# The state products of a group in one run, and padded decay tiles, in a Mamba-2 and attention trunk

## The chip, the cores and the metric

The kernel runs on one core of one Trainium2 chip. The metric is the device time of one execution in microseconds (us); lower is better. The engines are called PE (TensorE, matrix products and transposes), DVE (VectorE), ACT (ScalarE), POOL (GpSimd) and SP (SyncE, which issues the transfers).

## The reference

The input x has 512 positions of 1024 channels. A Mamba-2 layer is followed by one K/V projection and a differential attention layer; all is float32. The change lies in the Mamba-2 layer, of which these lines matter (G = 8 groups, R = 4 heads a group, head dimension 64, state 128; the kernel uses chunks of 128 positions, so NQ = 4 of them):

```python
zxbcdt = rms_norm(x, norm_g) @ w_in            # z, x/B/C and dt
xbc = silu(causal_depthwise_conv(xbc, conv_w, conv_b))
dt = softplus(dt_raw + dt_bias)
# per chunk, per group:
acs = cumsum(a * dt);  decay = exp(where(causal, acs[l] - acs[s], -inf))
y_diag = einsum((C @ B.T) * decay, x * dt)
y_off  = einsum(C, state) * exp(acs)
state  = state * exp(acs[-1]) + einsum(B, x * dt * exp(acs[-1] - acs))
# after all chunks:
y = y_diag + y_off + d_skip * x
u = y * silu(z);  u = u * rsqrt(mean(u * u over the group) + EPS) * gate_norm_g
x = x + u @ w_out
```

## The kernel before, in words

**Dense products.** The projections go through PE as three products in place of one (`mm3`): a weight is split into a head `whi` (made on ACT, `head`, line 144) and a rest `wlo` (made on DVE, `rest`, line 150), an activation likewise (`a_hi`, `a_lo`; `yh`, `yl`), and whi x hi, wlo x hi and whi x lo are summed. One product is 128x512 or a part of it. The weights come in segments: z0 g0 g1 z1 g2 g3 z2 g4 o0 g5 z3 g6 g7 o1 o2 o3, where z is the gate, g one group's x, B and C, and o the out-projection of two groups, in two halves. Segments are fetched some ahead of their use. In the trace the products are named pz, pg and po with their four token blocks; those of an out-projection segment `o3`, first half, have the names po3_0_0 to po3_0_3 and take the weights whi30 and wlo30. The second half of o3 has the weights whi31 and wlo31, which are placed in the two buffers of the decays, tag "dec" (line 137).

**The scan.** `ssd(g)` (from line 567) does one group, with these steps: B times C of each chunk (pcb, PE); transposes of B and x (pbt, pxt, PE) and from them bt (ACT), xdt = x dt and dx = d_skip x (DVE); xe, xdt weighted to a chunk's end, for three chunks (POOL, line 595); the product of pcb and the decays (DVE, into `dec`); the state products psA (chunks 0 and 1) and psB (chunk 2), full float32, each shown as two records; from these the states hst, in turns of ACT, POOL and DVE; the products pyd within a chunk, 64 records; the products of C with the states, po1 (chunk 1) and po2 (chunks 2 and 3), which the trace names po<-hst,xc; tmp, these times exp(acs) (DVE); dx + tmp (POOL, line 644); the gating with zs (DVE); the squares for the mean (ACT, with a read of the accumulator each); v and a chain of nine small operations of 128x4 for the inverse root (DVE, names y_i, y_y, y_c); the scaling tmp<-dx,y_y (ACT, in group 7 half of it on DVE); the transposes pyt back (PE); yh (ACT) and yl (DVE), which are the out-projection's activation. The residual x_tok takes each finished block of po (DVE).

**What sets the order.** Each engine takes its instructions in one order, which is fixed when the program is built. `tile.TileContext` (with `schedule_with_timeline_sim=True`) merges the stream of dense segments with the instructions of `ssd(g)` by a simulated timeline. What is issued through the wrapper `Ordered` (line 45; `T` is PE's) while its `on` is set stays in the order in which it was written, relative to the others kept so; `ssd(7)` is issued with high priority. So a small edit in `ssd` can move many instructions on all engines. Tiles are placed by pools: `bp` and `bp2` hold those of the scan, and a tile of odd length shifts the place of those behind it. At the places of the diff the kernel has a tile `shift` of 96 floats in `bp2`, and `dec` has N_DEC = 2056 floats.

Of the kernel before, what the change touches and what calls it, by code (L numbers as in the profile page):

```python
# [9 lines left out]
F32 = mybir.dt.float32  # L10
F32R = mybir.dt.float32r
# [6 lines left out]
P = 128  # L18
# [21 lines left out]
N_PAR = 203  # L40

N_DEC = R * NQ * P + 2 * R


class Ordered:
# [18 lines left out]
def trunk(ctx, tc, x, x_t, par, w_dt, w_in, w_out, w_kvqg, w_bo, d_skip, lam_qk, fin_g, out):  # L64
    nc = tc.nc
    V, A, T = (Ordered(tc, e) for e in (nc.vector, nc.scalar, nc.tensor))
# [14 lines left out]
    def ss_bank(name):  # L81
        turns[0] += 1
        tag = "mm" if turns[0] % turns[1] >= 3 else "ss"
        return psum.tile([P, 512], F32, tag=tag, name=name, bufs=3 if tag == "ss" else 4)
# [22 lines left out]
    def source(seg):  # L107
        kind, a, b = seg
        if kind == "z":
            return w_in[a * 6 + b], [prm[:, C_GA + 4 * b + i:C_GA + 4 * b + i + 1] for i in range(4)]  # L110
        if kind == "g":
            return w_in[(a // 2) * 6 + 2 + (a % 2) * 2 + b], [prm[:, C_GA + 4 * b + i:C_GA + 4 * b + i + 1] for i in range(4)]
        if kind == "o":
            return w_out[a * 2 + b], [prm[:, C_GG + 4 * a + i:C_GG + 4 * a + i + 1] for i in range(4)]
        if kind in "bc":
            return w_bo[a], None
        name = f"v{a}" if kind == "v" else a
        at = C_GK if kind in "vk" else C_GB
        return w_kvqg[[i for i in ORDER_B if i[0] not in "bc"].index(name)], [prm[:, at + i:at + i + 1] for i in range(8)]
# [5 lines left out]
    def load(i):  # L125

        seg = segs[i]
        src, gains = source(seg)
        nk = 8 if seg[0] in "vkqt" else 4
        w = 2048 // nk  # L130
        raw = begun[i] if i in begun else wp.tile([P, nk, w], F32, tag="raw", name=f"raw{i}", bufs=2)
        fetched[0] += 1

        def split():

            pool, tags = (bp, ("dec", "dec")) if seg == ("o", 3, 1) else (wp, ("whi", "wlo"))
            if pool is bp:
                hi, lo = (pool.tile([P, N_DEC], F32R, tag=tag, name=f"{n}{i}", bufs=2)[:, 0:2048].rearrange("p (k n) -> p k n", k=nk)
                          for n, tag in zip(("whi", "wlo"), tags))
            else:  # L140
                hi, lo = (pool.tile([P, nk, w], F32R, tag=tag, name=f"{n}{i}", bufs=2) for n, tag in zip(("whi", "wlo"), tags))
            ready[seg] = (hi, lo)

            def head(k):
                if gains:
                    A.activation(hi[:, k, :], raw[:, k, :], AF.Copy, scale=gains[k])
                else:
                    A.copy(hi[:, k, :], raw[:, k, :])

            def rest(k):  # L150
                if gains:
                    V.scalar_tensor_tensor(out=lo[:, k, :], in0=raw[:, k, :], scalar=gains[k],
                                           in1=hi[:, k, :].bitcast(F32), op0=ALU.mult, op1=ALU.subtract)
                else:
                    V.tensor_tensor(out=lo[:, k, :], in0=raw[:, k, :], in1=hi[:, k, :].bitcast(F32), op=ALU.subtract)

            return [(head, rest, k) for k in range(nk)]

        if i == 0:

            nc.sync.dma_start(raw[:, 0, :], src[:, 0:w])
            for n in range(2):
                nc.sync.dma_start(xt[0][:, 0, n * 256:(n + 1) * 256], x_t[:, 0, n * 256:(n + 1) * 256])
            nc.sync.dma_start(raw[:, 1, :], src[:, w:2 * w])
            for n in range(2):
                nc.sync.dma_start(xt[0][:, 1, n * 256:(n + 1) * 256], x_t[:, 1, n * 256:(n + 1) * 256])
            for k in range(2, 4):
                nc.sync.dma_start(raw[:, k, :], src[:, k * w:(k + 1) * w])
                nc.sync.dma_start(xt[1][:, k - 2, :], x_t[:, k, :])

            nxt, (src1, _) = wp.tile([P, nk, w], F32, tag="raw", name="raw1", bufs=2), source(segs[1])
            begun[1] = nxt
            for i in range(2, 4):
                nc.sync.dma_start(xt[i], x_t[:, 2 * i:2 * i + 2, :])
                nc.sync.dma_start(nxt[:, 2 * i - 4:2 * i - 2, :].rearrange("p k n -> p (k n)"), src1[:, (2 * i - 4) * w:(2 * i - 2) * w])
            nc.sync.dma_start(prc[:], par[:, C_CB:N_PAR])
        elif i not in begun:
            nc.sync.dma_start(raw.rearrange("p k n -> p (k n)"), src)
        return split
# [177 lines left out]
    bp = bctx.enter_context(tc.tile_pool(name="bp", bufs=1))  # L357
    bp2 = bctx.enter_context(tc.tile_pool(name="bp2", bufs=2))

    bp2.tile([P, 96], F32, name="shift", bufs=1)  # L360

    zt = {}
    yT = {}
# [55 lines left out]
    for k in range(KD):  # L419
        for c in range(NQ):  # L420
            T.matmul(ps_dt[c * H:(c + 1) * H, 0:P], lhsT=dtw_raw[:, k, :], rhs=xt[k // 2][:, k % 2, c * P:(c + 1) * P],
                     start=k == 0, stop=k == KD - 1)
# [125 lines left out]
    def decays(gs):  # L548

        for g in gs:  # L550
            hs = slice(R * g, R * g + R)
            both = bp.tile([P, N_DEC], F32, tag="dec", name=f"dec{g}", bufs=2)
            dec = both[:, 0:R * NQ * P].rearrange("p (h c l) -> p h c l", h=R, c=NQ)
            een = both[:, R * NQ * P:].rearrange("p (h q) -> p h q", h=R)
            nc.sync.dma_start(both[:, 0:R * NQ * P],
                                acs_d[hs].rearrange("h c l -> (h c l)").partition_broadcast(P))
            GP.tensor_copy(een, dec[:, :, 1:3, P - 1])
            for h in range(R):
                GP.tensor_tensor(out=dec[:, h], in0=dec[:, h], in1=acs_tok[:, :, R * g + h].unsqueeze(2).to_broadcast([P, NQ, P]), op=ALU.subtract)
                GP.affine_select(out=dec[:, h], in_=dec[:, h], compare_op=ALU.is_ge, fill=-BIG, base=0,  # L560
                                 pattern=[[0, NQ], [1, P]], channel_multiplier=-1)
            decs[g] = (dec, een, both)

        for g in gs:
            A.activation(decs[g][2], decs[g][2], AF.Exp)

    def ssd(g):
        bc, cc, x0, x1 = conv_out.pop(g)
        xc = (x0, x1)
        dec, een, _ = decs.pop(g)  # L570
# [29 lines left out]
        hsf = hst.rearrange("p c h e -> p c (h e)")  # L600
        psA = ss_bank(f"psA{g}")
        T.on = True
        for c in range(2):
            T.matmul(psA[:, c * 256:(c + 1) * 256], lhsT=bt[:, c, :], rhs=xe[:, c].rearrange("p h e -> p (h e)"), start=True, stop=True)
        A.copy(hsf[:, 0], psA[:, 0:256])
        GP.tensor_tensor(out=hst[:, 1], in0=hst[:, 0], in1=een[:, :, 0:1].to_broadcast([P, R, HD]), op=ALU.mult)
# [21 lines left out]
        if g % 2 and g < G - 1:  # L628
            decays((g + 1, g + 2))

        po1 = ss_bank(f"po1{g}")
        T.matmul(po1[:, 256:512], lhsT=cc[:, P:2 * P], rhs=hsf[:, 0], start=True, stop=True)
        po2 = ss_bank(f"po2{g}")
        for c in (2, 3):
            T.matmul(po2[:, (c - 2) * 256:(c - 1) * 256], lhsT=cc[:, c * P:(c + 1) * P], rhs=hsf[:, c - 1], start=True, stop=True)
        V.tensor_tensor(out=tmp[:, 1], in0=po1[:, 256:512].rearrange("p (h e) -> p h e", e=HD),
                        in1=eacs_tok[:, 1, hs].unsqueeze(2).to_broadcast([P, R, HD]), op=ALU.mult)
        V.tensor_tensor(out=tmp[:, 2:4], in0=po2.rearrange("p (c h e) -> p c h e", h=R, e=HD),
# [20 lines left out]
        n = 2 if g == G - 1 else NQ  # L659
# [6 lines left out]
        yT[g] = (yh, yl)  # L666

    decays((0, 1))
    dense[0] = stream_a()
    for g in range(G):  # L670
        until(f"g{g}")
        if g < G - 1:
            ssd(g)
        else:
            with tc.high_priority():
                ssd(g)
# [282 lines left out]
    def half(t, n):  # L959
        hs = slice(n * 512, (n + 1) * 512)  # L960
        return x_tok[:, t, hs], fg[:, hs], ot[t][:, hs], out[t * P:(t + 1) * P, hs]
# [123 lines left out]
    y, f, o, dst = half(3, 0)  # L1085
# [8 lines left out]
    y, f, o, dst = half(3, 1)  # L1094
# [68 lines left out]
```

## Time and profile before

| | before |
|---|---|
| median of 3 runs | 709.59 us (709.17 to 709.61) |
| profiled execution | 709.26 us |
| its span (first to last instruction) | 707.5 us |
| instructions | 10916 |
| PE busy | 697.5 us, 99% |
| DVE / ACT / POOL busy | 519.5 / 430.1 / 111.7 us |

The times of the profile count from the start of the span. A row of a timeline has the start, the duration of the whole row, the engine, the line and operation, the tile written and the tiles read with the buffer numbers left out, the shapes and a count of like instructions in sequence; a bracket names idle time before the row and what ended it. Matmuls overlap: a step is read from one start to the next, not from a duration. All operations that go through a recording helper have one line, 55 in the kernel before and 56 after.

### The profile page before, as it was taken

How to read it: one execution, taken by the hardware profiler on the slowest of the kernel's cores; microseconds unless marked ns; L12 is line 12 of the kernel's file. 1: busy time of each engine (PE TensorE's matmuls, PEld its weight loads, DVE VectorE, ACT ScalarE, POOL GpSimd, SP SyncE). 2: the span in 40 equal slices, each digit the busy share in tenths (PEclk: the TensorE clock that was granted, in tenths of full speed). 3: DMA queues.
4: the chain of work that ended last, by engine and by line, in shares of the span. 5: the costliest groups of instructions: out<-in, count | busy, mean ns of one | idle time of the engine just before them, and what ended most of it. 6: DMA issues, size and time to landing. Idle time of an engine off the chain costs nothing.

```text
span 707.5 us, 10916 instructions
## 1 busy us (share of the span) xinstructions
PE 697.5 (99%) x4030; PEld 590.8 (84%) x4030; DVE 519.5 (73%) x1197; ACT 430.1 (61%) x955; POOL 111.7 (16%) x158
## 2 busy tenths in 40 slices
PE   9999999999999999999999999999999999999996
PEld 7777888888888888888888879888988998899885
DVE  5479964889579569568997856566767757785886
ACT  6739672764744537538535367676667766756556
POOL 0009421503306024050110101000000000000002
PEclk9999999999999999999999999999999999999999
DMA  8644313333133331331221311412211221122003
GB/s 303 246 151 152 120 59 127 113 120 120 60 119 120 120 120 60 119 120 59 73 100 68 120 60 36 152 60 93 87 61 60 75 105 59 61 101 80 31 0 120
DMA packets 13493, 70.88 MB, mean 100 GB/s; under 512 B 1792, under 2 KB 3328, under 8 KB 6016
## 3 DMA queue, kind: packets, MB, share of 16 engines
q1 hardware_dynamic: 13008, 69.90, 27.6%
q8 instruction: 32, 0.52, 0.3%
q10 hardware_dynamic: 432, 0.28, 0.1%
q14 instruction: 21, 0.17, 0.1%
HBM read 68.02 MB, written 2.16 MB: 99 GB/s over the span
## 4 chain that ended last, share of the span: by engine, by line
PE 88%; ACT 4%; DVE 3%; DMA 3%; issue 1%; SPq 0%; ACTq 0%; DVEq 0%
PE pg L55 20%; PE po L55 16%; PE pz L55 9%; PE pt L55 7%; PE pv L55 6%; PE pq L55 6%; PE pk L55 6%; PE pb L55 3%; DMA raw<-in_w_in 3%; PE sc L55 3%; PE pyd L55 2%; PE pc L55 2%; ACT whi L55 1%; PE pxt L55 1%; PE psA L55 1%; PE pyt L55 1%
## 5 line engine op out<-in xcount | busy, mean ns | idle before, releaser
L55 DVE SCALAR_TENSOR_TENSOR wlo<-raw,prm,whi 128x512 fp32r<-128x512 f32 (+1 forms) x256 | 150.8, 637 | 56.1 <-ACT whi L55 55.6
L55 ACT ACTIVATE whi<-raw,prm 128x512 fp32r<-128x512 f32 (+1 forms) x256 | 136.8, 607 | 62.8 <-issue 13.1
L55 PE MATMUL pg<-a_hi,whi 128*128 128x512 f32 x256 | 102.2, 399 | 0.4 <-ACT zs L55 0.3
L55 PE MATMUL pg<-a_lo,whi 128*128 128x512 f32 x256 | 101.1, 395 | 0.0
L55 PE MATMUL pg<-a_hi,wlo 128*128 128x512 f32 x256 | 100.0, 396 | 0.0
L55 DVE SCALAR_TENSOR_TENSOR xc<-pg,prc,xc 128x511 f32<-128x511 f32 (+2 forms) x96 | 69.9, 739 | 7.5 <-ACT xc L55 7.1
L55 PEld LDWEIGHTS pg<-a_hi,whi 128*128 128x128 f32 x256 | 48.1, 188 | 10.5 <-ACT zs L55 0.6
L55 PEld LDWEIGHTS pg<-a_hi,wlo 128*128 128x128 f32 x256 | 48.1, 188 | 9.8
L55 PEld LDWEIGHTS pg<-a_lo,whi 128*128 128x128 f32 x256 | 48.1, 188 | 9.6
L55 PE MATMUL po<-whi,yh 128*128 128x512 f32 x128 | 50.8, 397 | 0.4 <-ACT yh L55 0.4
L55 PE MATMUL po<-wlo,yh 128*128 128x512 f32 x128 | 50.8, 397 | 0.0
L55 PE MATMUL po<-whi,yl 128*128 128x512 f32 x128 | 50.1, 395 | 0.0
L55 PE MATMUL pz<-wlo,a_hi 128*128 128x512 f32 x128 | 49.3, 394 | 0.0
L55 PE MATMUL pz<-whi,a_hi 128*128 128x512 f32 x128 | 48.9, 396 | 0.0
L55 PE MATMUL pz<-whi,a_lo 128*128 128x512 f32 x128 | 48.8, 390 | 0.0
L968 POOL TENSOR_TENSOR ot<-x_tok,fg 128x512 f32<-128x512 f32 x4 | 5.0, 1290 | 246.4 <-DVE x_tok L55 246.4
L55 ACT ACTIVATE s<-s,mx 128x128 f32<-128x128 f32 (+3 forms) x64 | 35.5, 556 | 9.7 <-DVE mx L55 9.3
L55 ACT ACTIVATE xc<-pg,prc 128x512 f32<-128x512 f32 x32 | 24.8, 776 | 24.5 <-DVE pg L55 19.6
L595 POOL TENSOR_TENSOR xe<-xdt,tok 128x256 f32<-128x256 f32 x24 | 14.1, 614 | 161.5 <-DVE xdt L55 161.5
L55 DVE CUSTOM_DVE_ANT_0 s<-sc,bias 128x128 f32<-128x128 f32 (+3 forms) x64 | 29.3, 487 | 12.3 <-PE sc L55 11.8
L55 PE MATMUL pv<-whi,b_hi 128*128 128x256 f32 x128 | 36.9, 289 | 0.0
L55 PE MATMUL pv<-whi,b_lo 128*128 128x256 f32 x128 | 36.2, 283 | 0.0
(238 smaller groups left out, 1676.5 us busy)
## 6 DMA issues: line engine op xcount, KB each, us to landing
raw<-in_w_in SPq DMA_DIRECT2D x22, 1024.0 KB, 4.9
raw<-in_w_kvqg SPq DMA_DIRECT2D x16, 1024.0 KB, 4.8
dec<-acs_d SPq DMA_DIRECT2D x8, 1024.0 KB, 4.8
raw<-in_w_out SPq DMA_DIRECT2D x8, 1024.0 KB, 4.7
raw<-in_w_bo SPq DMA_DIRECT2D x4, 1024.0 KB, 4.7
x_tok<-in_x SPq DMA_DIRECT2D x4, 512.0 KB, 9.0
out<-ot SPq DMA_DIRECT2D x6, 256.0 KB, 2.3
raw<-in_w_in SPq DMA_DIRECT2D x4, 256.0 KB, 4.7
```

Source lines behind the costliest of these rows:

```text
L55: i = op(*args, **kw)
L595: GP.tensor_tensor(out=xe[:, c], in0=xdt[:, c], in1=toe_tok[:, c, hs].unsqueeze(2).to_broadcast([P, R, HD]), op=ALU.mult)
L968: GP.tensor_tensor(out=o, in0=y, in1=f, op=ALU.mult)
```

## The change

Four edits:

- the state products are issued as chunk 1 then chunk 0 (psA), and po2 (chunk 3, then 2) is issued ahead of po1, these three now inside a stretch that is kept in written order;
- the decays' tiles get 2176 floats in place of 2056, of which the same 2056 are used; o3's second half in the same buffers too;
- the tile `shift` has 112 floats in place of 96 and moves from the pool `bp2` to `bp`;
- the argument dynamic_dma_scratch_size of the program is 1024 where it had its default, which moves the tiles by 15360 bytes a partition.

```diff
+N_DEC_PAD = 2176
...
-                hi, lo = (pool.tile([P, N_DEC], F32R, tag=tag, name=f"{n}{i}", bufs=2)[:, 0:2048].rearrange("p (k n) -> p k n", k=nk)
+                hi, lo = (pool.tile([P, N_DEC_PAD], F32R, tag=tag, name=f"{n}{i}", bufs=2)[:, 0:2048].rearrange("p (k n) -> p k n", k=nk)
...
-    bp2.tile([P, 96], F32, name="shift", bufs=1)
+    bp.tile([P, 112], F32, name="shift")
...
-            both = bp.tile([P, N_DEC], F32, tag="dec", name=f"dec{g}", bufs=2)
+            both = bp.tile([P, N_DEC_PAD], F32, tag="dec", name=f"dec{g}", bufs=2)[:, 0:N_DEC]
...
-        for c in range(2):
+        for c in (1, 0):
             T.matmul(psA[:, c * 256:(c + 1) * 256], lhsT=bt[:, c, :], rhs=xe[:, c].rearrange("p h e -> p (h e)"), start=True, stop=True)
...
+        po2 = ss_bank(f"po2{g}")
+        T.on = True
+        for c in (3, 2):
+            T.matmul(po2[:, (c - 2) * 256:(c - 1) * 256], lhsT=cc[:, c * P:(c + 1) * P], rhs=hsf[:, c - 1], start=True, stop=True)
         po1 = ss_bank(f"po1{g}")
         T.matmul(po1[:, 256:512], lhsT=cc[:, P:2 * P], rhs=hsf[:, 0], start=True, stop=True)
-        po2 = ss_bank(f"po2{g}")
-        for c in (2, 3):
-            T.matmul(po2[:, (c - 2) * 256:(c - 1) * 256], lhsT=cc[:, c * P:(c + 1) * P], rhs=hsf[:, c - 1], start=True, stop=True)
+        T.on = False
...
-    nc = bacc.Bacc("TRN2", target_bir_lowering=False, num_devices=1)
+    nc = bacc.Bacc("TRN2", target_bir_lowering=False, num_devices=1, dynamic_dma_scratch_size=1024)
```

By the addresses of the tiles, counted modulo 512 bytes, the two buffers of dec go from 192 and 224 to 128, and with them whi31 and wlo31; bt, xdt, dx, xe, hst and tmp go from 256 to 128; the other tiles of the products stay where they are, most of them at 128.

PE in group 7, before: the state products psA7 and psB7, pyd7 and po17 between products of the out-projection (po2_1_1 is its third segment's second half, second token block).

```order
L55 MATMUL psA7_3378<-xe7_3369,bt7_3351 128x256
L55 MATMUL po2_1_1_3696<-whi29_3536,yl4_2283 128x512
L55 MATMUL psA7_3378<-xe7_3369,bt7_3351 128x256
L55 MATMUL po2_1_1_3696<-whi29_3536,yh4_2282 128x512
L55 MATMUL psB7_3384<-xe7_3369,bt7_3351 128x256
L55 MATMUL pyd7_1_3391<-xdt7_3353,dec7_2692 64x64 x16
L55 MATMUL pyd7_0_3390<-xdt7_3353,dec7_2692 64x64 x16
L55 MATMUL po17_3426<-hst7_3377,xc31_3281 128x256
L55 MATMUL po2_1_1_3696<-wlo29_3537,yh4_2282 128x512
```

The same place after:

```order
L56 MATMUL po2_1_2_3710<-whi29_3536,yl5_2750 128x512
L56 MATMUL psA7_3378<-xe7_3369,bt7_3351 128x256 x2
L56 MATMUL psB7_3384<-xe7_3369,bt7_3351 128x256
L56 MATMUL pyd7_1_3391<-xdt7_3353,dec7_2692 64x64 x16
L56 MATMUL pyd7_0_3390<-xdt7_3353,dec7_2692 64x64 x16
L56 MATMUL po2_1_2_3710<-whi29_3536,yh5_2749 128x512
```

psA7's two products and psB7 stand together, and all of it stands 19 dense products further back in the out-projection.

PE at the products with the states, group 7, before: po27 alone, po17 having stood 15 dense products earlier. 41 dense products follow it up to the first pyt7.

```order
L55 MATMUL po2_1_2_3710<-whi29_3536,yh5_2749 128x512
L55 MATMUL po27_3428<-hst7_3377,xc31_3281 128x256 x2
L55 MATMUL po2_1_2_3710<-wlo29_3537,yh5_2749 128x512
L55 MATMUL po2_1_2_3710<-whi29_3536,yl5_2750 128x512
L55 MATMUL po2_1_2_3710<-whi29_3536,yh5_2749 128x512
```

After: the three products stand together behind the first two products of po3_0_0, and 22 dense products follow up to the first pyt7.

```order
L56 MATMUL po2_1_3_3724<-whi29_3536,yl5_2750 128x512
L56 MATMUL po3_0_0_3758<-whi30_3604,yh6_3177 128x512
L56 MATMUL po3_0_0_3758<-wlo30_3605,yh6_3177 128x512
L56 MATMUL po27_3426<-hst7_3377,xc31_3281 128x256 x2
L56 MATMUL po17_3429<-hst7_3377,xc31_3281 128x256
L56 MATMUL po3_0_0_3758<-whi30_3604,yl6_3178 128x512
```

The first pyt7 stands behind the same products in both; what comes behind it on PE needs yh7 or yl7.

DVE behind group 7's products with the states, before (zs3 is the gate, x_tok the residual):

```order
L55 TENSOR_TENSOR tmp7_3389<-po17_3426,tok_438 128x256
L55 TENSOR_TENSOR x_tok_73<-po2_1_1_3696,x_tok_73 128x512
L55 TENSOR_TENSOR dx7_3354<-dx7_3354,zs3_0_1_2836 128x256
L55 TENSOR_TENSOR dx7_3354<-dx7_3354,zs3_1_1_2852 128x256
L55 TENSOR_TENSOR tmp7_3389<-po27_3428,tok_438 128x512
L55 TENSOR_TENSOR x_tok_73<-po2_1_2_3710,x_tok_73 128x512
L55 TENSOR_TENSOR dx7_3354<-dx7_3354,zs3_2_1_2868 128x256
L55 TENSOR_TENSOR dx7_3354<-dx7_3354,zs3_3_1_2884 128x256
L55 TENSOR_SCALAR v47_3444<-ss47_3388 128x4
L55 TENSOR_TENSOR x_tok_73<-po2_1_3_3724,x_tok_73 128x512
L55 TENSOR_SCALAR y_i_3448<-v47_3444 128x4
```

After:

```order
L56 TENSOR_TENSOR x_tok_73<-po2_1_2_3710,x_tok_73 128x512
L56 TENSOR_TENSOR x_tok_73<-po2_1_3_3724,x_tok_73 128x512
L56 TENSOR_TENSOR dx7_3354<-dx7_3354,zs3_0_1_2836 128x256
L56 TENSOR_TENSOR tmp7_3389<-po27_3426,tok_438 128x512
L56 TENSOR_TENSOR tmp7_3389<-po17_3429,tok_438 128x256
L56 TENSOR_TENSOR dx7_3354<-dx7_3354,zs3_2_1_2868 128x256
L56 TENSOR_TENSOR dx7_3354<-dx7_3354,zs3_3_1_2884 128x256
L56 TENSOR_TENSOR dx7_3354<-dx7_3354,zs3_1_1_2852 128x256
L56 TENSOR_SCALAR v47_3444<-ss47_3388 128x4
L56 TENSOR_SCALAR y_i_3448<-v47_3444 128x4
```

Chunk 1's tmp and gating have moved to the end of the group, and the residual adds to its front. Behind y_i the order is the same in both: the rest of the chain, three wlo32, the two scalings tmp7, five wlo32, yl7. On ACT the eight whi32 stood behind group 7's four squares before and stand ahead of them after. SP's order is the same.

## The prediction, made before the changed kernel had run

> **What bounds the kernel now.** I read the busy lines and the chain of the page first, then who TensorE (PE) waits for, then the timelines of PE and of the engines that feed it where the change moves something.
>
> ```profile
> span 707.5 us, 10916 instructions
> PE 697.5 (99%) x4030; PEld 590.8 (84%) x4030; DVE 519.5 (73%) x1197; ACT 430.1 (61%) x955; POOL 111.7 (16%) x158
> PE 88%; ACT 4%; DVE 3%; DMA 3%; issue 1%; SPq 0%; ACTq 0%; DVEq 0%
> PE warm L55 <- POOL ident masks.py:199: 1.5, 1, 1.5
> PE pxt L55 <- ACT xc L55: 1.4, 1, 1.4
> PE po L55 <- ACT yh L55: 0.4, 1, 0.4
> PE pg L55 <- ACT zs L55: 0.3, 1, 0.3
> ```
>
> PE is busy for 99% of the span, makes 88% of the chain that ended last, and in the whole program waits four times, 3.6 us together. The two long ones are for POOL's ident and ACT's xc, which the change leaves alone, and the others are too short to matter. So time can be won in two ways only: PE's own instructions become shorter or fewer, or one of those waits goes. It is lost as soon as PE, which takes its instructions in the written order, meets one whose input isn't there. The change alters no count of matmuls; what it alters is their neighbours, their addresses and, through the scheduler, who stands in front of whom.
>
> **Part one: products in one run.** A run of two state products of po, with dense products around it:
>
> ```profile
> 126.18 0.39 PE L55 MATMUL pg<-a_hi,wlo 128*128 128x512 f32 x1
> 126.41 1.02 PE L55 MATMUL po<-hst,xc 128*128 128x256 f32 x4
> ...
> 127.50 0.40 PE L55 MATMUL pg<-a_lo,whi 128*128 128x512 f32 x1
> 127.97 0.40 PE L55 MATMUL pg<-a_hi,whi 128*128 128x512 f32 x1
> ...
> 133.90 0.39 PE L55 MATMUL pg<-a_hi,wlo 128*128 128x512 f32 x1
> 388.30 0.60 PE L55 MATMUL psA<-xe,bt 128*128 128x256 f32 x2
> ...
> 388.96 0.59 PE L55 MATMUL psA<-xe,bt 128*128 128x256 f32 x2
> ...
> 389.62 0.59 PE L55 MATMUL psB<-xe,bt 128*128 128x256 f32 x2
> ```
>
> From the start at 127.97 to that at 133.90 lie 26 dense steps, 228 ns each. A state product is two records (x2). In group 7 psA to psA takes 0.66 us with one dense product between: 0.66 - 0.228 leaves 0.43 for two records, 0.216 each. The run of four with the dense product behind it goes from 126.41 to 127.50, 1.09 us; 4 x 0.216 + 0.228 is 1.09. Entering and leaving a run therefore costs no more than the rounding, some 10 to 20 ns. About 14 runs disappear (psA is split in most groups, po in most): 0.15 us gained, and 0 to 0.3 are its ends. This is all that comes of "together" on PE itself.
>
> **Part two: the padding.** It moves dec, bt, xdt, dx, xe, hst and tmp to 128 modulo 512 (dec from 192 and 224, the others from 256), and with dec the second half of out-projection segment o3, whose weights live in dec's buffers.
>
> ```profile
> 413.37 0.40 PE L55 MATMUL po<-whi,yh 128*128 128x512 f32 x1
> ...
> 421.51 0.41 PE L55 MATMUL po<-whi,yl 128*128 128x512 f32 x1
> ```
>
> These are 36 dense products, 35 steps from start to start: 8.14 / 35 = 232.6 ns, where the steps of 127.97 to 133.90 took 228. I read these 5 ns as the price of weights at 192 and 224. The segment has 48 products: 48 x 5 ns, about 0.25 us gained, with 0 and 0.3 as ends. [...]
>
> For the small products, pyd, I have no row with other places:
>
> ```profile
> 390.15 2.08 PE L55 MATMUL pyd<-xdt,dec 128*64 128x64 f32 x64
> 392.16 0.70 PE L55 MATMUL po<-hst,xc 128*128 128x256 f32 x2
> ```
>
> 2.01 us a group for 64 records. At worst nothing changes; at best each pair of records gains the 5 ns above: 32 x 8 x 5 ns = 1.3 us, and the 96 records of psA, psB and po 0.5 more. I take 0: a record of psA (bt and xe at 256) and one of po (hst at 256, xc where it stays) both cost 0.216 us, so the place doesn't show there. The smaller scratch moves every tile by 30 x 512 bytes and so alters no place, and SP's order, with all its transfers, is the same row for row: 0 for both.
>
> **Part three: the order, group 7.** Here the change costs. Before, po's last two products of group 7 are followed by 41 dense products and then by the transposes pyt, which need the gated, normed y. All other work of PE before these pyt is the same in both orders. After, the run of three stands behind two products of segment o3, and only 22 dense products are left to put between it and pyt; the remaining ones need y itself. PE before:
>
> ```profile
> 396.14 1.02 PE L55 MATMUL po<-hst,xc 128*128 128x256 f32 x4
> ...
> 406.35 0.60 PE L55 MATMUL pyt<-ident,tmp 128*128 128x128 f32 x4
> 407.30 0.50 PE L55 MATMUL po<-whi,yh 128*128 128x512 f32 x1 [0.35 <-ACT yh L55]
> ...
> 408.47 0.48 PE L55 MATMUL po<-whi,yl 128*128 128x512 f32 x1
> ```
>
> Call the run's start X (396.14). Before, PE reaches pyt 10.21 us after X. After, it has 6 records (1.30) and 22 dense products (5.0): it reaches pyt at X+6.3, and X itself lies 3.9 later. What must happen between, by the rows of before:
>
> ```profile
> 396.04 0.73 POOL L644 TENSOR_TENSOR dx<-dx,tmp 128x256 f32<-128x256 f32 x1 [4.23 <-DVE tmp L55]
> 397.30 0.68 DVE L55 TENSOR_TENSOR tmp<-po,tok 128x512 f32<-128x512 f32 x1
> 398.06 1.43 POOL L644 TENSOR_TENSOR dx<-dx,tmp 128x256 f32<-128x256 f32 x2 [1.29 <-DVE tmp L55]
> 398.97 1.13 DVE L55 TENSOR_TENSOR dx<-dx,zs 128x256 f32<-128x256 f32 x2
> 400.22 0.40 ACT L55 ACTIVATE tmp<-dx 128x256 f32<-128x256 f32 x1
> 401.16 3.31 ACT L55 ACTIVATE whi<-raw,prm 128x256 fp32r<-128x256 f32 x8 [0.44 <-ACT tmp L55]
> 400.75 0.17 DVE L55 TENSOR_SCALAR v<-ss 128x4 f32<-128x4 f32 x1 [0.64 <-ACT tmp L55]
> 401.72 0.16 DVE L55 TENSOR_SCALAR y_i<-v 128x4 int32<-128x4 int32 x1
> 401.91 0.17 DVE L55 TENSOR_SCALAR y_y<-y_i 128x4 int32<-128x4 int32 x1
> 403.38 1.27 DVE L55 SCALAR_TENSOR_TENSOR wlo<-raw,prm,whi 128x256 fp32r<-128x256 f32 x3
> 404.57 0.61 DVE L55 TENSOR_SCALAR tmp<-dx,y_y 128x256 f32<-128x256 f32 x2
> 405.10 2.06 DVE L55 SCALAR_TENSOR_TENSOR wlo<-raw,prm,whi 128x256 fp32r<-128x256 f32 x5
> 407.28 0.75 DVE L55 TENSOR_TENSOR yl<-pyt,yh 128x256 fp32r<-128x256 f32 x2
> ```
>
> tmp starts at X+1.16 (397.30), POOL's add at X+1.92 (398.06). Before, one of the three adds was long done (396.04); after, all three stand behind the run, 1.43 / 2 = 0.71 each, so POOL ends at X+4.06. The last gating ended 0.61 behind POOL's last add (400.10 against 399.49), v began 0.65 behind that: X+5.32. The residual add between v and the y chain has moved ahead of the gating, so y_i starts one such small step later (401.72 to 401.91), X+5.52. From y_i to the scaling tmp<-dx,y_y went 2.85 us (401.72 to 404.57), with three wlo operations among it, which keep their place: X+8.37. The first scaling takes half of 0.61 and some 0.1 to be seen: pyt can start at X+8.8. PE is there at X+6.3. **It stands for 2.5 us.** ACT doesn't decide: its eight whi operations (3.31 us) move ahead of the squares, and as the buffer that they fill is read for the last time right before X, they end by X+3.3, ahead of the last square.
>
> Then yl. It comes 2.71 behind the scaling (404.57 to 407.28), five wlo operations being between: X+11.08, its first half done at about X+11.5. PE, from pyt to the product with yl, needs 2.12 (406.35 to 408.47): X+10.9. **Another 0.6 us.** Behind it nothing is waited for in before, so nothing gives the 3.1 us back. Ends: if the gating and adds run at the shorter halves of their rows (0.2 us off each of three links), 2.5; if DVE and POOL, which now alternate for three adds instead of two, disturb each other more, the row is
>
> ```profile
> L55 DVE TENSOR_TENSOR dx<-dx,zs 128x256 f32<-128x256 f32 x32 | 16.9, 534 | 1.8 <-POOL dx L644 1.7
> ```
>
> 534 ns in the mean, 565 in the two of the tail (1.13 / 2). One more of them between adds of 0.71 may wait out up to one such add: 3.8 at most. [...]
>
> **The other groups** have no such end: scan and projections of other groups remain to be put between. The tightest is group 2, where pyt moves ahead by 23 dense products while the state products move back:
>
> ```profile
> 193.54 1.71 ACT L55 ACTIVATE tmp<-dx,y_y 128x256 f32<-128x256 f32 x4
> 196.24 1.03 PE L55 MATMUL pyt<-ident,tmp 128*128 128x128 f32 x8
> ```
>
> Its scaling ended 1.0 us ahead of pyt, but behind whi and zs operations that move with it. I take 0 and keep 2 us as the other end.
>
> **The sum.** The profiled execution took 709.26 (span 707.5 and 1.8 around it); the median is 709.59, 0.33 more. 709.26 - 0.15 - 0.25 + 3.1 = 711.9; on the median, 712.2.
>
> **Rivals.**
> - The tail is covered: PE meets pyt when y is there, because X comes earlier than the order says or the chain behind it is shorter. For it: PE idles nowhere in this stage today but for 0.35 us. Against: y would have to come in 6.3 us, where the rows add to 8.8. Then only parts one and two act: 709.59 - 0.4 = 709.2. No change. Chance 0.17.
> - Faster: the places weigh on the fp32 products too, and the tail is covered. 709.2 - 1.3 to 1.8, about 707.6. It decides if a pair of pyd's records loses over 4 ns (4 x 256 is 1.0, and 709.2 - 1.0 is 708.2, the bound of "faster"). Against it stands the equal price of psA and po. Chance 0.08. (With the tail's stall it would be 710.5.)
> - Slower still: group 2, or another with its run moved back, stalls as well: 712.2 + 1 to 2, about 713.7. For it: the 1.0 us there. Chance 0.17.
> - The change does nothing, if order and places had no weight: 709.6. The moved rows make this unlikely; 0.03.
>
> **How the numbers follow.** The forecast is 712.2 with chance 0.55; its own range, from 2.5 to 3.8 us of stall with the ends of the gains, is 711.5 to 713.4 (709.6 - 0.6 + 2.5, and 709.6 - 0 + 3.8). With the places weighing on pyd besides, it goes down to 710.5; with another group's stall up to 714.2. To leave out no more than 2 in 10 the range must take in the covered tail too: 709.0 to 714.2, which leaves out the faster case and the outermost stalls. A measurement of this kernel can tell about 0.2% (1.4 us) from no change, so slower means over 711.0: the forecast and the further stalls, less a little for the forecast's low end, 0.71. Same: the covered tail, the change without weight and that low end, 0.21. Faster: 0.08.
>
> **What would show it.** Right: in the profile after, PE waits for tmp at pyt once, by 2 to 3 us, near 406.3, and for yl by 0.5 to 1; the last stretch of o3 steps at 227 ns; runs of psA x4 and po x6 that cost 0.216 a record. Wrong: no wait at pyt of group 7, a wait elsewhere, pyd under 1.95 us a group, or steps of 232 ns still there.

## The result, and the profile after

The changed kernel takes 716.28 us in the median of six runs (714.03 to 717.24), the kernel before 709.6 beside it: a ratio of 1.0091 (95% interval 1.0078 to 1.0104), so it is slower, and by more than forecast (712.2, range 709.0 to 714.2). The profiled execution is the fastest of the six, 714.03 us with a span of 712.3.

Of the kernel after, the page, and then the list of what PE waited for (total, times, longest):

```profile
span 712.3 us, 10923 instructions
PE 698.2 (98%) x4030; PEld 591.6 (83%) x4030; DVE 526.9 (74%) x1197; ACT 429.7 (60%) x955; POOL 117.5 (17%) x158
PE 80%; DVE 7%; ACT 5%; DMA 3%; issue 2%; POOL 1%; SPq 1%; ACTq 0%; POOLq 0%; DVEq 0%
```

```profile
PE pyt L56 <- ACT tmp L56: 1.6, 1, 1.6
PE warm L56 <- POOL ident masks.py:199: 1.5, 1, 1.5
...
PE pz L56 <- ACT whi L56: 0.9, 1, 0.9
PE po L56 <- DVE xc L56: 0.8, 1, 0.8
PE pyt L56 <- DVE yl L56: 0.6, 1, 0.6
PE po L56 <- ACT tmp L56: 0.5, 1, 0.5
PE pyt L56 <- DVE tmp L56: 0.4, 1, 0.4
PE po L56 <- ACT yh L56: 0.4, 1, 0.4
```

PE's own busy time is that of before within 0.7 us. What is new are waits: 7.8 us together where there were 3.6, and the chain has 80% on PE where it had 88%. Three of the new rows belong to group 7's first transposes, as forecast. Three do not: pz, po for "xc" and po for "tmp".

**The tail of group 7.** PE and then DVE in the kernel after:

```profile
401.76 1.46 PE L56 MATMUL po<-hst,xc 128*128 128x256 f32 x6
...
403.28 0.39 PE L56 MATMUL po<-whi,yh 128*128 128x512 f32 x1
...
409.82 0.44 PE L56 MATMUL pyt<-ident,tmp 128*128 128x128 f32 x2 [1.59 <-ACT tmp L56]
410.67 0.44 PE L56 MATMUL pyt<-ident,tmp 128*128 128x128 f32 x2 [0.41 <-DVE tmp L56]
411.46 0.50 PE L56 MATMUL po<-whi,yh 128*128 128x512 f32 x1 [0.35 <-ACT yh L56]
...
413.24 0.44 PE L56 MATMUL pyt<-ident,tmp 128*128 128x128 f32 x2 [0.59 <-DVE yl L56]
413.44 0.48 PE L56 MATMUL po<-whi,yl 128*128 128x512 f32 x1
```

```profile
404.40 2.16 DVE L56 TENSOR_TENSOR dx<-dx,zs 128x256 f32<-128x256 f32 x3 [0.52 <-POOL dx L647]
407.40 0.17 DVE L56 TENSOR_SCALAR y_i<-v 128x4 int32<-128x4 int32 x1
410.26 0.61 DVE L56 TENSOR_SCALAR tmp<-dx,y_y 128x256 f32<-128x256 f32 x2
412.77 0.75 DVE L56 TENSOR_TENSOR yl<-pyt,yh 128x256 fp32r<-128x256 f32 x2
```

With X = 401.76, the start of the run, y_i comes at X+5.64 (forecast 5.52), DVE's scaling at X+8.50 (8.37), the transposes of its chunk at X+8.91 (8.8), yl at X+11.01 (11.08), the product with yl at X+11.68. By PE's own work it would have stood at X+8.4 (6.3 + 2.12). The tail costs 3.3 us; 3.1 was forecast. The wait at the transposes came in two, 1.59 and 0.41 us: the first two of them need ACT's scaling alone and start at X+8.06, which the forecast had left out. The run itself: six records and a product from 401.76 to 403.28, 1.52 us, against 6 x 0.216 + 0.228 = 1.52. It is as cheap as the prediction said.

**Three waits for a bank.** In the kernel after, PE at the starts of segment z2, of o0's second half and of o1, and then what DVE did there:

```profile
160.39 0.47 PE L56 MATMUL pz<-whi,a_hi 128*128 128x512 f32 x1 [0.90 <-ACT whi L56]
...
229.24 0.47 PE L56 MATMUL po<-whi,yh 128*128 128x512 f32 x1 [0.51 <-ACT tmp L56]
...
346.14 0.47 PE L56 MATMUL po<-whi,yh 128*128 128x512 f32 x1 [0.81 <-DVE xc L56]
```

```profile
158.90 0.70 DVE L56 TENSOR_TENSOR pg<-pg,ar_row 128x512 f32<-128x512 f32 x1
159.50 0.74 DVE L56 SCALAR_TENSOR_TENSOR xc<-pg,prc,xc 128x509 f32<-128x509 f32 x1
...
228.41 0.68 DVE L56 TENSOR_TENSOR x_tok<-po,x_tok 128x512 f32<-128x512 f32 x1
...
345.26 0.74 DVE L56 SCALAR_TENSOR_TENSOR xc<-pg,prc,xc 128x509 f32<-128x509 f32 x1
```

The tiles of the dense products share four PSUM buffers, the banks (`mm_bank` in the kernel); the first product of a tile has to wait until the tile that had its bank before has been read. The releasers named in the brackets had long been done; each time PE starts 0.14 or 0.15 us after DVE's last read of an earlier PSUM tile (160.25, 229.09, 346.00). By tile names these are pg3_0, po0_0_1 and pg7_0. In the program as built, PE waits at each of these three starts for just this DVE instruction, and the new tile has the bank of the tile that is read. The lag is 0.15 us again in the other profile of this kernel, where the first wait is 0.6 us longer, so it is DVE's read that lets PE go. At z2 and o1 DVE has, in the new order, one operation more between its reads of the tile (at z2 the row at 158.90). In the kernel before, the three reads had ended 0.76, 1.50 and 0.75 us before PE came, at 160.28, 228.41 and 344.38. Here is the first, DVE and then PE (the third of DVE's operations, the read of pg3_0, ends at 159.53):

```profile
157.48 2.05 DVE L55 SCALAR_TENSOR_TENSOR xc<-pg,prc,xc 128x510 f32<-128x510 f32 x3
```

```profile
160.28 0.39 PE L55 MATMUL pz<-whi,a_hi 128*128 128x512 f32 x1
```

**The padding.** The second half of o3 in the kernel after, 36 products:

```profile
418.33 0.39 PE L56 MATMUL po<-whi,yh 128*128 128x512 f32 x1
...
426.27 0.39 PE L56 MATMUL po<-whi,yl 128*128 128x512 f32 x1
```

7.94 / 35 = 226.9 ns a step, against 232.6 before. The product pyd is unchanged.

**Where the time went.** PE's lateness is the start of a product less the sum of the steps of all that PE does ahead of it. Its difference to before, in us, by place. Ahead of the tail, behind it and behind o3 PE has done the same work in all orders, so the difference there is that of the starts themselves. The columns are the changed kernel's profile and those of five experiments below, each one execution:

| place | after | after again | places only | order only | groups 1, 3 old | no norm in 7 |
|---|---|---|---|---|---|---|
| ahead of z2 | -0.9 | -0.3 | +0.5 | -0.3 | +0.1 | 0.0 |
| behind z2's start | +0.2 | +1.4 | +0.5 | +1.5 | +0.1 | +1.8 |
| behind o0's second half's start | +0.9 | +2.1 | +0.4 | +2.8 | +0.2 | +3.0 |
| behind o1's start | +1.9 | +3.0 | +0.5 | +3.8 | +1.1 | +3.9 |
| ahead of the tail (group 7's first transposes) | +1.7 | +2.9 | +0.5 | +3.7 | +1.0 | +3.7 |
| behind the tail | +5.0 | +6.6 | +0.5 | +7.0 | +5.2 | +5.3 |
| behind o3 | +4.7 | +6.3 | +0.3 | +7.0 | +5.0 | +5.0 |

In the changed kernel's own profile the four new waits make 1.1 + 0.7 + 0.9 + 3.3; the rest is 0.25 us back in o3 and an early part that differs from one execution to the next.

### The profile page after: what moved, and what is told of

Same layout as the page of the kernel before. It is cut to its first block, busy times and chain, and to the rows that moved or that the text cites. A ratio compares the mean times of both kernels' runs of the same rounds, so it can differ in the third digit from the quotient of the medians.

```text
span 712.3 us, 10923 instructions
## 1 busy us (share of the span) xinstructions
PE 698.2 (98%) x4030; PEld 591.6 (83%) x4030; DVE 526.9 (74%) x1197; ACT 429.7 (60%) x955; POOL 117.5 (17%) x158
## 4 chain that ended last, share of the span: by engine, by line
PE 80%; DVE 7%; ACT 5%; DMA 3%; issue 2%; POOL 1%; SPq 1%; ACTq 0%; POOLq 0%; DVEq 0%
PE pg L56 17%; PE po L56 13%; PE pz L56 9%; PE pt L56 7%; PE pv L56 6%; PE pq L56 6%; PE pk L56 6%; PE pb L56 3%; PE sc L56 3%; PE pc L56 2%; DVE wlo L56 2%; PE pyd L56 2%; ACT whi L56 2%; DMA x_tok<-in_x 1%; DVE xc L56 1%
## 5 line engine op out<-in xcount | busy, mean ns | idle before, releaser
L56 DVE SCALAR_TENSOR_TENSOR wlo<-raw,prm,whi 128x512 fp32r<-128x512 f32 (+1 forms) x256 | 153.2, 648 | 56.8 <-ACT whi L56 56.5
L56 PE MATMUL pg<-a_hi,whi 128*128 128x512 f32 x256 | 100.7, 395 | 0.0
L596 POOL TENSOR_TENSOR xe<-xdt,tok 128x256 f32<-128x256 f32 x24 | 16.8, 727 | 156.6 <-DVE xdt L56 156.6
```

The costliest lines, as they stand in the source:

```text
L56: i = op(*args, **kw)
L596: GP.tensor_tensor(out=xe[:, c], in0=xdt[:, c], in1=toe_tok[:, c, hs].unsqueeze(2).to_broadcast([P, R, HD]), op=ALU.mult)
```

## The experiments

**Places alone, order alone.** The diff of the change, cut in two. Places only has the lines on N_DEC_PAD, shift and the scratch; order only has these:

```diff
-        for c in range(2):
+        for c in (1, 0):
             T.matmul(psA...)
...
+        po2, then po1, between T.on = True and T.on = False
```

> Only the padding of dec, the moved shift tile and the smaller scratch; the order of every engine is that of before, row for row. Theory A (the order loses the time, the places gain a little): 0.25 us faster than before, 709.3, the waits of TensorE as before (3.6 us together), the steps of o3's second half 227 ns in place of 232, pyd as before. Rival B (the places themselves make DVE and POOL slower, as DVE is busy 7.4 us more and POOL 5.8 us more in the changed kernel, and the waits follow from that): at least 1 us slower than before, DVE busy 523 or more in place of 519.5.

> Only the two edits of the order (psA's chunks turned round, po2 ahead of po1 in a kept stretch); the order of every engine is that of the changed kernel, row for row, the places are those of before. Theory A: 0.25 us slower than the changed kernel in like executions, so 714.3 in an execution with a granted clock of 0.999 and about 716.5 in the median; the same waits of TensorE (7.8 us together, 3 of them for the weights' and projections' banks, 3.5 in group 7's tail); o3's second half at 232 ns. Rival B: most of the loss gone, 710 to 712.

Places only: 709.17 us, ratio 0.9989 (0.9975 to 1.0003). Order only: 716.88 us, ratio 1.0099 (1.0085 to 1.0113). The busy lines of places only and then of order only:

```profile
PE 698.0 (99%) x4030; PEld 591.2 (84%) x4030; DVE 520.2 (73%) x1197; ACT 430.3 (61%) x955; POOL 113.4 (16%) x158
```

```profile
PE 698.2 (98%) x4030; PEld 590.8 (83%) x4030; DVE 527.9 (74%) x1197; ACT 430.1 (60%) x955; POOL 118.3 (17%) x158
```

The whole loss is the order's, and so are DVE's 7 to 8 and POOL's 5 us of busy time: the counts of operations are the same (x1197 and x158), so each takes longer; no run shows why. Rival B falls. The places give the forecast 0.25 us in o3 (from +0.5 to +0.3 in the table), which the times can't tell from nothing.

**The changed kernel again.**

> The changed kernel once more. Its six times went from 714.0 to 717.2 while the granted clock fell from 0.999 to 0.995. Theory C (a lower clock of TensorE for some us behind group 7's tail, in some executions): the median is again 2 us above the fastest, time and clock go together, with the span longer by about (0.999 - clock) x span, and a profile of an execution below 0.998 shows the low clock in one stretch between 405 and 420 us. Rival D (noise of the chip, as much in the kernel before): before shows the same spread and the same clocks.

715.66 us (715.16 to 716.18), clocks 0.995 and 0.996. The spread of 2 us did not come back; all four executions have the low clock. It isn't foreign to the kernel before, but rare there: 3 of the 64 executions beside this and the later runs have 0.995 or less. TensorE's granted clock in this profile by stretches of 1 us (start and end, length, PE busy, clock, DMA), and two steps of PE in it:

```profile
409.00:410.00 1.00, 0.37 (x2) 1.00 0.00 0
410.00:411.00 1.00, 0.04 (x1) 1.00 0.00 0
411.00:412.00 1.00, 0.58 (x3) 0.90 0.00 0
412.00:413.00 1.00, 0.75 (x3) 0.50 0.00 0
...
414.00:415.00 1.00, 1.00 (x5) 0.50 0.00 0
415.00:416.00 1.00, 1.00 (x6) 0.89 0.57 131
```

```profile
413.34 0.63 PE L56 MATMUL po<-wlo,yh 128*128 128x512 f32 x1
413.77 0.63 PE L56 MATMUL po<-whi,yh 128*128 128x512 f32 x1
```

Right behind the tail's waits the clock is 0.50 for 3.4 us (0.2 + 3 + 0.22), and a dense step takes 0.43 us in place of 0.23. The profile of the first run shows no such stretch before the program's end, where the clock falls at 710.18. Theory C stands for this stretch.

PE had been busy for 1.42 of the 3.41 us right ahead of the fall (408.39 to 411.80). In the first profile it is busy for only 1.04 of 3.4 us in the same tail (408.2 to 411.6), and the clock stays at 1.00. So the same tail can be hit or not; what decides it no run shows.

From the start of o3 to that of its second half the first profile takes 17.03 us and this one 17.48, so the stretch cost 0.45 us. The two executions differ by 1.62; 0.6 of it stands ahead of z2 and 0.6 is the longer wait at z2.

**Scaling in group 7 turned.**

```diff
-            if g == G - 1 and c % 2:
+            if g == G - 1 and c >= 2:
```

> The changed kernel, but in group 7 ACT scales chunks 0 and 1 and DVE chunks 2 and 3 (it was 0 and 2, and 1 and 3); all engines keep their order. The first transposes then hang on ACT alone. Theory A2 (the tail's end is set by yl, which stands behind five wlo operations on DVE): the wait of the first transposes for DVE's scaling goes (0.4 us) and comes back as a longer wait for yl; total unchanged within 0.2 us. Rival (each wait adds): 0.4 to 0.5 us faster than the changed kernel.

717.36 us (714.69 to 719.07), no gain, but 1.7 us more than the changed kernel beside it. In its profile the wait for DVE's scaling is gone and that for yl grew from 0.6 to 0.8, as A2 said; but the clock was then 0.50 for 6.8 us, twice as long as above, so the time alone decides little.

**Needless work in the tail.**

```diff
         pyt = [ss_bank(f"pyt{g}_{j}") for j in range(2)]
+        if g == G - 1:
+            for _ in range(5):
+                T.matmul(pyt[0][:, 0:256], lhsT=ident, rhs=u[:, 1], start=True, stop=True)
```

> The changed kernel with five needless products of 128x256 float32 (0.43 us each) on TensorE right ahead of group 7's first transposes, where it stands idle for 1.8 us; they read a chunk that is ready by then and are written over by the transposes. Nothing else moves. Theory C (the low clock is TensorE's answer to the idle time of the tail): no clock below 0.998, the median falls to the changed kernel's fast executions, 714 to 714.8, though work was added. Rival D (the low clocks are the chip's noise): median as the changed kernel's or longer, 715.7 to 717.5, clocks again down to 0.995.

Clocks of 0.997 to 0.999 in all five executions, but 716.51 us (714.56 to 717.79): the low clock went and the median did not fall. In its profile the waits at z2 and o0 had grown to 1.5 and 1.6 us. Half of the expectation fails; the next pair was made to settle it, on the kernel with groups 1 and 3 as before, which lacks those two waits (it is told below):

> The kernel of run_not_in_groups_1_and_3 once more, to stand beside the next one on the same chip. Theory C: most executions below a clock of 0.997, median near 714.3, fastest near 713.0.

> The same kernel with the five needless products ahead of group 7's first transposes. No bank waits at z2 and o0 disturb the comparison here. Theory C (TensorE's clock is halved for 3.4 us or twice that when the tail leaves it idle): no execution with a clock of 0.996 or less, median 0.7 to 1.5 us below the kernel without the products, 712.8 to 713.6. Rival D (the low clocks come by themselves, or from other places): clocks of 0.995 again and a median within 0.4 us of the other or above it.

Without the products 713.96 us (clocks 0.995 to 0.997), with them 712.77 (clocks 0.997 to 0.999), the ranges 713.34 to 714.78 and 712.24 to 713.41. Clocks in the profiles, first without, then with the needless work:

```profile
409.00:412.00 3.00, 2.10 (x7) 0.72 0.00 0
412.00:416.00 4.00, 4.00 (x18) 0.79 0.71 229
```

```profile
409.00:412.00 3.00, 2.00 (x10) 1.00 0.00 0
412.00:416.00 4.00, 4.00 (x20) 1.00 0.67 262
```

More work on PE, and 1.2 us less time in the median. So PE's idle time in the tail brings the low clock, where an execution has it. Its price is smaller than that: of the 1.26 us between the two profiled executions 0.77 already stand ahead of o3 (its start is at 400.72 and 399.95), where the two programs are the same; from there to the start of o3's second half they take 17.53 and 17.05 us. Measured by this length one low stretch costs 0.45 to 1.0 us (17.48, 17.53 and, in the run of groups 1 and 3 as before, 18.01, against 17.03). The mean clock alone is a rough sign: both profiled executions have 0.997, and only the first has the stretch.

**Group 7 alone in the new order.** The places are the changed ones here and in all kernels below but the two that have one edit alone.

```diff
-        for c in (1, 0):
+        for c in ((1, 0) if g == G - 1 else (0, 1)):
...
+        if g == G - 1:
             po2, po1 in a kept run
+        else:
+            po1, po2 as before
```

> Places as changed; psA turned round and po2, po1 in one run only in group 7, groups 0 to 6 as before. The run stands 9.9 us of TensorE's work ahead of the first transposes, against 6.3 in the changed kernel. Theory A3 (the tail stalls by the chain from the run to the transposes, 8.9 us, less TensorE's work between): no wait at the transposes, no bank waits, 709.2 as places_only. Rival E (the run itself lengthens the tail, since POOL's three adds now stand behind one another): 1 us or more slower than places_only, 710.2 or more, with a wait at the transposes.

709.23 us, ratio 1.0000 (0.9992 to 1.0009). PE in its group 7:

```profile
390.53 1.02 PE L56 MATMUL psA<-xe,bt 128*128 128x256 f32 x4
...
397.92 1.46 PE L56 MATMUL po<-hst,xc 128*128 128x256 f32 x6
407.85 0.60 PE L56 MATMUL pyt<-ident,tmp 128*128 128x128 f32 x4
```

Both runs are there, 9.93 us lie between the run and the transposes, and PE doesn't wait. The run in group 7 costs nothing; what cost in the changed kernel is that the whole group had slid 19 products back. Rival E falls. One part of the expectation fails: in this profile, of an execution of 710.55 us, PE waits 1.1 us for a bank at 139.05, in segment g3, where the order is that of before. A bank wait can come in the old order too, in some executions.

**Each edit alone, all groups**, with the places of before.

> Before with only psA's chunks turned round in all groups; places as before. In group 7 the last run stands 9.0 us of TensorE's work ahead of the first transposes. Theory A3: a wait there of at most 0.3 us. The bank waits at the starts of segments (three in the changed kernel, 2.7 us): those at z2 go, since psA of group 2 stands ahead of that segment's start here (it had moved behind it), the others may stay. In all 709.5 to 711.5. Rival B2 (psA's turn is the whole loss): 714 or more.

> Before with only po2 ahead of po1 in a kept stretch, all groups; places as before. The run stands 9.2 us of TensorE's work ahead of the first transposes of group 7. Theory A3: no wait at them over 0.3 us. psA of group 2 stands as before, so the bank wait at z2 should go; the bank waits at the starts of o0's and o1's parts are open. In all 709.5 to 711.5. Rival B3 (the run of po is the whole loss): 714 or more.

Both expectations fail. psA alone: 720.05 us (718.21 to 727.28), more than both edits together; its profile has the wait at z2 that was to go, 1.3 us, and 1.4, 0.4 and 0.6 us at group 7's transposes. po alone: 714.05 us (712.85 to 715.02), with 1.4 and 0.4 us of wait at group 7's transposes, though the run stands 9.2 us ahead of them. ACT there, the squares of chunks 3 and 1 with whi between (the accumulator reads left out):

```profile
403.81 0.40 ACT L55 ACTIVATE tmp<-dx 128x256 f32<-128x256 f32 x1
...
404.22 2.49 ACT L55 ACTIVATE whi<-raw,prm 128x256 fp32r<-128x256 f32 x6
406.62 0.40 ACT L55 ACTIVATE tmp<-dx 128x256 f32<-128x256 f32 x1
```

The last square waits out six whi operations that this order puts ahead of it: they make 2.4 us. The transposes of the chunk that DVE scales come at 11.7 us behind the run, 2.8 more than the 8.9 that theory A3 took for fixed. The chain's length is the order's too, on each engine that it passes. In the profile of psA alone (the slowest of its six executions), DVE and then POOL near 60 us:

```profile
57.99 8.24 DVE L55 SCALAR_TENSOR_TENSOR wlo<-raw,prm,whi 128x512 fp32r<-128x512 f32 x1
```

```profile
58.09 1.22 POOL L560 TENSOR_SCALAR_AFFINE_SELECT dec<-dec 128x512 f32<-128x512 f32 x2
59.27 4.07 POOL L559 TENSOR_TENSOR dec<-dec,tok 128x512 f32<-128x512 f32 x4
63.30 2.39 POOL L560 TENSOR_SCALAR_AFFINE_SELECT dec<-dec 128x512 f32<-128x512 f32 x4
```

One DVE operation wlo<-raw,prm,whi, 0.79 us in the mean of 128 in before, takes 8.24 us and ends at 66.23, 0.5 us behind a stretch of ten POOL operations without a gap. PE waits 4.6 us for it, and from 65.8 to 72.6 the clock is 0.50 (in the mean 0.58 from 65 to 70 and 0.74 from 70 to 75). That explains much of this execution; the other five (718 to 722) were not profiled.

**Group 7 without its norm.** Squares, mean and inverse root are left out for group 7, whose y is scaled by a constant instead.

```diff
-            A.activation(tm[:, c], u[:, c], AF.Square, accum_out=ss4[:, c:c + 1])
+            if g < G - 1:
+                A.activation(tm[:, c], u[:, c], AF.Square, accum_out=ss4[:, c:c + 1])
...
-        r4 = rsqrt(v4, NQ, "y")
+        r4 = rsqrt(v4, NQ, "y") if g < G - 1 else dsk
```

> The changed kernel without group 7's squares, mean, inverse root (its y is scaled by a constant instead, so the output differs). TensorE's order is the changed kernel's, row for row; on DVE the eight wlo operations of the next segment move ahead of the gating. The chain from the run to the first transposes should shorten from 8.9 to about 6.9 us, and yl has no wlo operation ahead of it; TensorE's work between is 6.3. Theory A (the tail's stall is that chain): 0.5 us of wait in the tail in place of 3.3, no stretch of low clock there, 711.3 to 712.8, the bank waits at z2, o0 and o1 still there. Rival F (something else in the tail, as the run itself or the clock by its own): 714 or more.

714.42 us (712.99 to 715.56). By its time the run lands where rival F was put, at 714 or more, and not at 711.3 to 712.8. The table tells why: its tail costs 1.5 us where the changed kernel's cost 3.3, with PE's order the same, but 0.5 was expected, and its three bank waits make 3.9 us in this execution. The one wait left is for DVE's scaling:

```profile
PE pyt L56 <- DVE tmp L56: 1.3, 1, 1.3
```

The transposes of DVE's chunk came 8.0 us behind the run and not 6.9: the eight wlo operations now stood ahead of the gating on DVE. So more than half of the tail went with the norm, and I had the new length of the chain wrong by 1.1 us.

**Groups 1 and 3 as before.** The condition of the diff for group 7 is `g not in (1, 3)`.

> The changed kernel, but groups 1 and 3 have psA and po as before. The orders of all engines differ from the changed kernel's only from group 1 to group 4; o1's start and group 7's tail have the changed kernel's order. Theory G (each wait hangs on the order round it): the bank waits at z2 (1.1) and at o0's second half (0.7) go, that at o1 (1.0) and the tail's 3.3 with its low clock stay: 712.0 to 714.5, 1.8 less than the changed kernel. Rival H (waits come from the runs themselves, or from lateness that is carried along): all waits as in the changed kernel, or the later ones grow by what the earlier ones gave.

714.30 us (713.02 to 716.17). In the table, z2 and o0 cost nothing, o1 0.9 and the tail 4.2 with a clock of 0.66 in the mean from 410 to 415: each wait goes or stays with the order round it, and nothing is carried over. Theory G.

**Group 1 alone** (`g == 1`), **and groups 0, 2, 4, 6 and 7.**

> Before with the changed places, and the new psA and po in group 1 alone. It moves TensorE's instructions from group 1 to the end of the layer (psA of group 2 stands behind the start of z2, as in the changed kernel), though only two products change places by the edit. In group 7 the last run stands 10.8 us of TensorE's work ahead of the first transposes. Theory G: the wait at z2 is there (1.0 to 1.7), perhaps that at o0, the tail's is not: 710.3 to 712. Rival H: 709.2, as one group's run costs a seventh of the whole at most.

> Before with the changed places, and the new psA and po in groups 0, 2, 4, 6 and 7, where they leave the order of the rest nearly as before (126 rows of difference on TensorE against 526). Theory G: none of the four waits; the runs' own gain of 0.1 us and the places' 0.25: 709.0 to 709.3, within the noise of before. Rival H: five eighths of the loss, 712 or more.

Group 1 alone: 713.03 us (712.31 to 715.02), ratio 1.0052 (1.0032 to 1.0072). Its new waits:

```profile
PE po L56 <- DVE x_tok L56: 1.2, 1, 1.2
...
PE pz L56 <- DVE xc L56: 0.8, 1, 0.8
```

z2's is there, o0's and the tail's are not, and another, 1.2 us at 353.96, has come, so it is a microsecond above what I expected. In this program the second token block of o1 gets the bank of the block right before it, and waits for its residual; before, it had the bank of pg7_1. So the order also sets which bank a tile gets. The five groups together: 709.42 us, ratio 1.0004 (0.9985 to 1.0022): the runs in five of eight groups, and no loss. Its profile, of an execution of 710.39 us, has none of the four waits. Rival H falls by both.

## Why the prediction was wrong, point by point

- **The products together** were to gain 0.15 us. A run does cost its records and nothing else (1.52 us for six and a dense product). The gain was never seen: five groups with runs and padding stand at 1.0004. No more than the bound, and perhaps nothing.
- **The padding** was right: 226.9 in place of 232.6 ns a step, 0.25 us; pyd unchanged, as taken.
- **The tail of group 7** was right in mechanism and size (3.3 against 3.1 us), link by link within 0.2 us.
- **"The other groups: I take 0 and keep 2 us as the other end"** is the step that failed. I followed each group's data through the chain to pyt and found slack, which was there: no pyt of groups 0 to 6 waits. I never asked for the banks. At the start of each segment PE needs a PSUM bank back, and DVE, whose order had been changed as much as PE's, reads it later: 2.7 us in the first profile, 3.4 and 4.1 in two others with the same order. My rival on group 2 came near in size (1 to 2 us) by luck: its wait, at group 2's transposes, did not come, and the banks' waits stand elsewhere.
- **What an idle PE costs later** was missing. I priced the tail as lost time alone; in many executions (six of ten have a clock of 0.996 or less) the clock also falls behind it, in the profiles to 0.50 for 3.4 us (changed kernel) or 6.8 us (scaling turned). By the length of the tail in the profiles one such stretch costs 0.45 to 1.0 us.
- **From the profiled execution to the median** I added the 0.33 us that before shows. The changed kernel's median lies 2.2 us above its profiled execution, as its waits and its clock differ from run to run. The sum as written also adds to 712.3 and not 712.2, which changes nothing.

The sum as it was: 709.3 + 3.3 (tail) + 2.7 (banks) - 0.25 - 1.0 (early part and rest) = 714.0 in the profiled execution, and up to 3 us more in others. For one execution nearer the median, the 715.65 us of the second profile, the 1.6 us more are 0.6 ahead of z2, 0.6 at z2 and 0.45 of clock. What stays open: how the 2.2 us divide in the executions without a profile, and why the part ahead of z2 differs. In the first six runs time and clock fall together (714.03 at 0.999, 717.24 at 0.995), but fill_the_tail has 717.79 at 0.998, which the clock can't explain.

## What to carry to other kernels

Where a scheduler lays the order, a small edit is two changes: the edit, which here is worth a few tenths, and a new order of everything behind it, which cost 3 to 11 us each time that it was new and nothing where it stayed nearly as it was. So look first at how far the order moves, try the edit where it moves least, and in a new order check for every product at which PE changes banks, not only for the data chain, who reads that bank last and when. A wait on a PE that is otherwise always busy should be priced with the clock behind it, here 0.45 to 1.0 us for a stretch of 3.4 us.

## What the runs showed of the hardware

- TensorE's clock fell to 0.50 for 3.4 us (second profile of the changed kernel) or 6.8 us (scaling in group 7 turned) behind the tail's waits, of which the longest single one was 1.6 us: in the second profile with PE busy for 0.99 of the 3 us from 409 to 412 (0.37, 0.04 and 0.58). In the first profile, with the same waits and PE busy for 1.04 of the 3.4 us from 408.2 to 411.6, it did not fall; what decides it was not found.
- A DVE operation wlo<-raw,prm,whi of 128x512 took 8.24 us, in one execution, beside a gapless stretch of ten POOL operations, where the mean of before is 0.79 us; whether they held it up was not shown.
- Weights at 192 and 224 modulo 512 bytes took 232.6 ns a dense step and those at 128 took 227, in both orders; no other place was tried.
